# First layer's modulation rows loaded from GpSimd's queue, and the second half's first convolution weights split one step earlier

## The chip, the cores and the metric

One NeuronCore of a Trainium2 chip runs the whole program. The metric is the device time of one execution in microseconds (us), the median over several executions. TensorE is PE in the profile, VectorE is DVE, ScalarE is ACT, GpSimd is POOL, and SyncE, which here only issues DMAs, is SP. The letter q behind an engine's name (ACTq, SPq) marks what its queue does beside its computing: issuing a DMA or waiting on a semaphore.

## The reference

A two-layer decoder trunk over 1024 tokens of width 1024, in float32. Each layer is a token mixer and a squared-ReLU feed-forward network. Before each of them the residual stream is normalized (RMSNorm), scaled and shifted, and its result is gated. Scale, shift and gate come from a conditioning vector: `mod = silu(c) @ ada_w[i] + ada_b[i]`, six rows of 1024 for each layer. The first layer's mixer, the part that matters here, is

```python
u = h @ w_in                              # 1024 -> 2 x 1280
xb, gb = jnp.split(u, 2, axis=-1)
xc = causal_conv(xb, width 4) + conv_b
r, i = sigmoid(blockwise xc @ wr + br), sigmoid(blockwise xc @ wi + bi)
a = exp(-8 * r * softplus(-lam)); b = sqrt(1 - a*a) * (i * xc)
hs = scan(h_t = a_t * h_{t-1} + b_t)
y = (hs * gelu(gb)) @ w_out
```

## The kernel before, in words

**Tiling.** The 1024 tokens are two halves of 512, called h = 0 and h = 1. Activations lie transposed: a tile has 128 features on the partitions and 512 tokens along the row, 256 KB. Such tiles come from one pool of 54 buffers (tag `a`), which holds the residual stream, the mixer's inputs, the conv outputs, the mixer's outputs and the rows of `ada_w` on their way through.

**Products in three parts.** For float32 accuracy each operand is split in a high and a low part (`wh`, `wl` for weights). `mm3` (lines 343 to 347) issues three matmuls: high by high on line 345, high by low on 346, low by high on 347.

**Weights.** `weights` (line 299) loads a 512 KB block into one of three `raw` buffers over SP's queue (line 319), rounds it to `wh` on ACT (line 322), and subtracts to get `wl` (line 328). In the first layer's mixer the subtraction runs on DVE. `wh` and `wl` have five buffers each.

**The mixer** (`mixer0`, line 604). Its steps are written out in `plan` (line 1341): `c` is the conv branch of one of five blocks of 256 features, `g` the gelu branch, `l` the recurrence, `o` a part of the output product; the next digits are the blocks, the last one is the half. So `c01` is the conv branch of block 0 for half 1. A `c` or `g` step takes its weights from `wcols` (two blocks, `q` 0 and 1) and does 48 matmuls in `proj`. `nB` applies the norm to half 1: eight times a DVE instruction on line 96, one of ACT on line 97 and one of DVE on line 98, which give the eight inputs that every later step of half 1 needs. In the list around the change the order is `o20`, `nB`, `l40`, `c01`, `g01`, `o340`.

**Modulation as filler.** Rows of `ada_w` are not multiplied on PE in the mixer. `ada` (line 424) cuts a chunk of 1024 columns in eight steps; a step loads two 256 KB tiles (line 435) and DVE multiplies them by one entry of the condition each and adds (line 450 for the first step, line 452 for the others); `fin` turns the sum (PE, line 459) and reduces it (DVE, line 460). Each load is asked for one step ahead of its use. `pump` takes one such step from a list after each step of `plan`, two after steps 1 to 3. Four chunks of the first layer run during the mixer (64 loads); six of the second layer run later, during the feed-forward network (96 loads).

**What sets the order.** The kernel's text gives each instruction its engine and its place in the program. A scheduler then fixes, when the program is built, the order of every engine's queue, taking the earliest instruction in the program that is ready by its own model. On the chip each queue runs in that fixed order. Buffers of one tag are given out in the order of the program.

Of the kernel before, what the change touches and what calls it, by code (L numbers as in the profile page):

```python
# [21 lines left out]
P = 128  # L22
# [174 lines left out]
class Trunk:  # L197
# [226 lines left out]
    def ada(self, l, j, gain=None):  # L424

        nc = self.nc
        m = self.const.tile([P, KT], FT, name=f"mod{l}{j}")
        self.mod[l, j] = m
        st = {}

        def load(k):
            for c in range(2):
                st[k, c] = self.tile()
                o = j * D + c * 512
                nc.scalar.dma_start(st[k, c], self.i["ada_w"][l, k * P:(k + 1) * P, o:o + 512])

        self.loads += [lambda k=k: load(k) for k in range(KT)]

        def mac(k):
            if k == 0:  # L440
                st["acc"] = [self.tile(), self.tile()]
            while (k, 0) not in st:
                self.loads.pop(0)()
            if self.loads:
                self.loads.pop(0)()
            s = self.cond[:, k:k + 1]
            for c in range(2):
                r, a = st.pop((k, c)), st["acc"][c]
                if k == 0:
                    nc.vector.tensor_scalar(a, r, s, None, op0=OP.mult)  # L450
                else:
                    nc.vector.scalar_tensor_tensor(a, r, s, a, op0=OP.mult, op1=OP.add)  # L452

        def fin():
            t = self.small([P, KT], "adat")
            for c in range(2):
                ps = self.ps()
                for b in range(4):
                    nc.tensor.transpose(ps[:, b * P:(b + 1) * P], st["acc"][c][:, b * P:(b + 1) * P], self.ident)
                nc.vector.tensor_reduce(t[:, c * 4:c * 4 + 4], ps.rearrange("p (b k) -> p b k", b=4),  # L460
                                        axis=AX.X, op=OP.add)
            if gain is None:
                nc.vector.tensor_tensor(m, t, self.ada_b(l, j), op=OP.add)
            else:
                t2 = self.small([P, KT], "adat")
                nc.vector.tensor_tensor(t2, t, self.ada_b(l, j), op=OP.add)
                nc.vector.scalar_tensor_tensor(m, t2, 1.0, gain, op0=OP.add, op1=OP.mult)

        return [lambda k=k: mac(k) for k in range(KT)], fin
# [134 lines left out]
    def mixer0(self, hx, g1, tail, first, plan):  # L604
        nc, V, A, G = self.nc, self.nc.vector, self.nc.scalar, self.nc.gpsimd
# [6 lines left out]
        def wcols(c0):  # L612
            return [self.weights(w_in[0, q * 512:(q + 1) * 512, c0:c0 + 256].rearrange("(k p) c -> p k c", p=P),
                                 [4, 256], ("in", c0, q) if c0 not in (0, DR, 256) else None) for q in range(2)]

        def proj(W, h):
            pd = self.pd()
            pss = [pd[:, 0], pd[:, 1]]
            for kt in range(KT):
                wh, wl = W[kt // 4]  # L620
                for j in range(2):
                    s = slice(j * P, (j + 1) * P)
                    self.mm3(pss[j], (wh[:, kt % 4, s], wl[:, kt % 4, s]), hx[h][kt], kt == 0, kt == KT - 1)
            return pss

        def conv(u, h, pss=None):
            pss = pss or proj(wcols(u * 256), h)
            for j in range(2):
                f = 2 * u + j
                y = self.tmp("xc")  # L630
                A.activation(y, pss[j], AF.Identity, bias=self.convb(f), scale=self.convw(3, f))
                if h == 0:
                    A.copy(halo[:, f], pss[j][:, HT - 3:HT])
                for k in range(3):
                    d = 3 - k
                    V.scalar_tensor_tensor(y[:, d:], pss[j][:, 0:HT - d], self.convw(k, f), y[:, d:],  # L636
                                           op0=OP.mult, op1=OP.add)
                if h:
                    V.tensor_tensor(y[:, 0:3], y[:, 0:3], edge[:, f], op=OP.add)
                yh, yl = self.tileR(), self.tileR()  # L640
                A.copy(yh, y)
                V.tensor_tensor(yl, y, yh.bitcast(FT), op=OP.subtract)
                xc[u, j], xcs[u, j] = y, (yh, yl)

        def edges():

            t = self.small([P, 10, 3], "edge", 1)
            for k in range(3):
                n = 3 - k
                w = self.col[:, 136 + 10 * k:146 + 10 * k].rearrange("p (f o) -> p f o", o=1).to_broadcast([P, 10, n])  # L650
                d = t[:, :, 0:n] if k else edge
                V.tensor_tensor(d, halo[:, :, k:3], w, op=OP.mult)
                if k:
                    V.tensor_tensor(edge[:, :, 0:n], edge[:, :, 0:n], d, op=OP.add)
# [72 lines left out]
        conv(0, 0, first[0])  # L727
        gate(0, 0, first[1])
        conv(1, 0, first[2])
        for k, step in enumerate(plan):  # L730
            if callable(step):
                step()
            else:
                us = [int(u) for u in step[1:-1]]
                {"c": conv, "g": gate, "l": lru, "o": oproj}[step[0]](us if step[0] == "o" else us[0], int(step[-1]))
                if step == "c40":
                    edges()
            self.pump(2 if k in (1, 2, 3) else 1)
# [513 lines left out]
    def run(self):  # L1252
        tc = self.tc
        mod = self.mod = {}
        N = {}
        hm, hf = {}, {}

        def pool(st, name, bufs):
            return st.enter_context(tc.tile_pool(name=name, bufs=bufs))

        def sqs(key):
            def tail(h, m):
                if m == 0:
                    N[key, h] = Norm(self, h)
                N[key, h].sq(m)
            return tail
# [7 lines left out]
        def run(gen):  # L1274
            for _ in gen:
                pass
# [32 lines left out]
        with ExitStack() as st:  # L1309
            self.tp = pool(st, "tmp0", 18)  # L1310
            macs, fin = self.ada(0, 2)
            self.fill += macs
            self.ada_fill([(0, 4, self.gffn(0)), (0, 3), (0, 5)])
            self.loads.pop(0)()

            def nB():
                hm[1] = N["m0", 1].apply(mod[0, 1], mod[0, 0])

            def nA():
                hf[0] = N["f0", 0].apply(mod[0, 4], mod[0, 3])  # L1320

            def bA():
                N["f0", 0].bc()

            def stat0():
                N["f0", 0].stat()

            def f1a():
                self.drain()
                F.load1(0)  # L1330
                F.f1(0, 0)

            def f1b():
                def bcB():
                    N["f0", 1].bc()
                    hf[1] = N["f0", 1].apply(mod[0, 4], mod[0, 3])

                F.load1(1)
                F.f1(1, 0, mid={4: lambda: N["f0", 1].stat(), 6: bcB})

            plan = [lambda: self.second(), "g10", "l00", "c20", "l10", "g20", "c30", fin, "o010", "l20", "g30", "c40",
                    "l30", "g40", lambda: N["m0", 1].bc(), "o20", nB, "l40", "c01", "g01", "o340", "l01", "c11", stat0, "g11", "c21", "l11",
                    "g21", "c31", "o011", "l21", "g31", "c41", "l31", "g41", bA, "o21", nA, "l41", f1a, "o341", f1b]
            self.mixer0(hm, lambda: mod[0, 2], sqs("f0"), first, plan)
            self.drain()
            self.lo = [1]


            F.g2, F.tail = mod[0, 5], tail
            self.ada_fill([(1, 1, self.gmix(1)), (1, 0), (1, 2), (1, 4, self.gffn(1)), (1, 3), (1, 5)])  # L1350
            F.load2(0, 0)
            f2 = F.f2_steps([0], 0)
            for _ in range(4):
                next(f2)
            F.f1(0, 1), F.f1(1, 1)
            F.load2(0, 1)
            run(f2)
            F.f2([0], 1)
            for p in range(NJ):
                if p:  # L1360
                    F.load2(p, 0), F.load2(p, 1)
                    for h in range(2):
                        F.f2([p], h)
                if p + 2 < NJ:
                    F.load1(p + 2)
                    F.f1(p + 2, 0), F.f1(p + 2, 1)
            self.drain()
            F.twice = range(NJ, F.NP)
            F.single(0, NJ)
# [68 lines left out]
        with ExitStack() as st:  # L1438
# [72 lines left out]
            early = self.store(1, 0)  # L1511
# [38 lines left out]
```

## Time and profile before

| | us |
|---|---|
| runs: median of three | 2551.33 (2551.26 to 2557.24) |
| the profiled execution, time | 2558.93 |
| the profiled execution, span | 2557.0 |
| PE busy | 2435.1 |
| DVE busy | 1502.1 |
| ACT busy | 1227.8 |
| POOL busy | 797.6 |

The span runs from the first to the last instruction of the profiled execution. PE is busy for 95% of it, so little is to be had but where PE stands idle. Times in the trace are counted from the span's start; the first layer's mixer lies between about 70 and 500 us. A wait is put down to the instruction that released it: `PE pd L347 <- DVE wl L328` says that a matmul of line 347 waited for a `wl` that DVE wrote on line 328.

### The profile page before, as it was taken

What the parts mean: (1) busy time and instruction counts of PE and PEld (TensorE: products, weight loads), DVE (VectorE), ACT (ScalarE), POOL (GpSimd) and SP (SyncE); (2) the same over time, 40 slices, a digit from 0 to 9 for tenths busy, and PEclk for the clock granted to TensorE, in tenths of its full rate; (3) what the DMA queues carried; (4) which work ended last, traced back from release to release, by engine and by line L of the source; (5) the groups of instructions that cost most, each with busy time, mean ns of one, the idle gap of its engine ahead of it and who ended that gap; (6) DMA issues with size and microseconds to landing.
All of it is one profiled execution on the core that took longest, in us unless ns stands there. A gap on an engine that the chain in (4) does not pass through costs nothing. (4 is left out here: it accounts for less than half of the span.)

```text
span 2557.0 us, 30862 instructions
## 1 busy us (share of the span) xinstructions
PE 2435.1 (95%) x10954; PEld 1965.4 (77%) x10954; DVE 1502.1 (59%) x2905; ACT 1227.8 (48%) x2180; POOL 797.6 (31%) x507
## 2 busy tenths in 40 slices
PE   7998999999999999999987999999998999999999
PEld 6776787777788888788776777888887777788887
DVE  5888775788643412566677876555558875321212
ACT  3656465521211233235456667768634974423322
POOL 1000000022221243230238822322326994334442
PEclk8999999999999999999998999999999999999999
DMA  8564675356311577654321522322330114323231
GB/s 262 194 226 167 208 238 188 99 178 222 126 42 42 178 276 269 217 192 177 136 87 42 189 67 67 107 74 91 106 125 1 34 42 140 107 91 99 86 104 58
DMA packets 212284, 342.52 MB, mean 134 GB/s; under 512 B 19658, under 2 KB 123298, under 8 KB 212130
## 3 DMA queue, kind: packets, MB, share of 16 engines
q1 hardware_dynamic: 183184, 295.29, 34.2%
q10 hardware_dynamic: 28946, 45.27, 5.4%
q8 instruction: 86, 1.41, 0.2%
q14 instruction: 68, 0.56, 0.1%
HBM read 274.97 MB, written 65.54 MB: 133 GB/s over the span
## 5 line engine op out<-in xcount | busy, mean ns | idle before, releaser
L328 POOL TENSOR_TENSOR wl<-raw,wh 128x1024 fp32r<-128x1024 f32 (+2 forms) x194 | 470.7, 2433 | 1186.2 <-ACT wh L322 1169.3
L322 ACT CAST wh<-raw 128x1024 fp32r<-128x1024 f32 (+2 forms) x296 | 305.1, 1033 | 615.3 <-PE ps L346 238.8
L345 PE MATMUL ps<-a,wh 128*128 128x512 f32 x1152 | 461.0, 403 | 15.2 <-DVE a L723 7.5
L346 PE MATMUL ps<-a,wh 128*128 128x512 f32 x1152 | 459.2, 399 | 1.5 <-POOL a L1173 1.2
L347 PE MATMUL ps<-a,wl 128*128 128x512 f32 x1152 | 458.2, 399 | 0.7 <-DMA wl<-part 0.7
L345 PE MATMUL pd<-a,wh 128*128 128x512 f32 x1072 | 431.2, 404 | 12.2 <-DVE xc L636 9.4
L347 PE MATMUL pd<-a,wl 128*128 128x512 f32 x1072 | 429.5, 401 | 10.2 <-DVE wl L328 10.2
L346 PE MATMUL pd<-a,wh 128*128 128x512 f32 x1072 | 430.2, 402 | 2.0 <-DVE a L98 2.0
L168 DVE SCALAR_TENSOR_TENSOR a<-ps,mod,a 128x512 f32<-128x512 f32 x352 | 259.7, 746 | 262.8 <-PE ps L347 262.1
L345 PEld LDWEIGHTS ps<-a,wh 128*128 128x128 f32 x1152 | 218.5, 190 | 71.1 <-DVE a L723 7.9
L347 PEld LDWEIGHTS ps<-a,wl 128*128 128x128 f32 x1152 | 218.3, 190 | 54.4 <-DMA wl<-part 1.8
L346 PEld LDWEIGHTS ps<-a,wh 128*128 128x128 f32 x1152 | 218.4, 190 | 54.0 <-POOL a L1173 2.3
L345 PEld LDWEIGHTS pd<-a,wh 128*128 128x128 f32 x1072 | 204.6, 191 | 63.2 <-issue 6.5
L347 PEld LDWEIGHTS pd<-a,wl 128*128 128x128 f32 x1072 | 204.8, 191 | 60.7 <-DVE wl L328 11.1
L346 PEld LDWEIGHTS pd<-a,wh 128*128 128x128 f32 x1072 | 205.3, 191 | 53.2 <-DVE a L98 3.4
L1141 POOL TENSOR_SCALAR s<-s,rr 128x128 f32<-128x128 f32 (+7 forms) x128 | 225.9, 1782 | 35.8 <-DVE rr L1139 25.2
L345 PE MATMUL ps<-hid,wh 128*128 128x512 f32 x512 | 204.9, 400 | 9.6 <-DVE a L168 6.8
L346 PE MATMUL ps<-hid,wh 128*128 128x512 f32 x512 | 203.6, 398 | 0.0
L347 PE MATMUL ps<-hid,wl 128*128 128x512 f32 x512 | 203.6, 398 | 0.0
L1019 ACT ACTIVATE signs<-sc,tc 128x384 int8<-128x384 f32 (+5 forms) x186 | 164.0, 882 | 77.3 <-DVE tc L1034 66.0
L452 DVE SCALAR_TENSOR_TENSOR a<-a,cond,a 128x512 f32<-128x512 f32 x140 | 113.5, 840 | 40.7 <-DMA a<-in_ada_w_dram 40.3
L146 DVE TENSOR_TENSOR a<-r,a 128x512 fp32r<-128x512 f32 x64 | 46.8, 754 | 141.7 <-ACT a L145 140.4
(271 smaller groups left out, 3684.1 us busy)
## 6 DMA issues: line engine op xcount, KB each, us to landing
raw<-in_ffn_w_dram SPq DMA_DIRECT2D x192, 512.0 KB, 3.7
a<-in_ada_w_dram ACTq DMA_DIRECT2D x160, 256.0 KB, 3.4
part<-wl SPq DMA_DIRECT2D x69, 512.0 KB, 3.2
wl<-part SPq DMA_DIRECT2D x69, 512.0 KB, 4.3
part<-wh SPq DMA_DIRECT2D x40, 512.0 KB, 2.8
wh<-part SPq DMA_DIRECT2D x40, 512.0 KB, 3.8
raw<-in_a_w_in_dram SPq DMA_DIRECT2D x34, 512.0 KB, 4.9
raw<-in_a_w_out_dram SPq DMA_DIRECT2D x20, 512.0 KB, 4.1
```

The lines of the kernel that those rows point to most:

```text
L146: nc.any.tensor_tensor(ql, r, qh.bitcast(FT), op=OP.subtract)
L168: nc.vector.scalar_tensor_tensor(xt, ps, self.g2[:, m:m + 1], xt, op0=OP.mult, op1=OP.add)
L322: nc.scalar.copy(wh, raw)
L328: eng.tensor_tensor(wl, raw, wh.bitcast(FT), op=OP.subtract)
L345: pe.matmul(out, wh, xh, start=start, stop=False)
L346: pe.matmul(out, wh, xl, start=False, stop=False)
L347: pe.matmul(out, wl, xh, start=False, stop=stop)
L452: nc.vector.scalar_tensor_tensor(a, r, s, a, op0=OP.mult, op1=OP.add)
L1019: A.activation(self.signs[:, 0:L], sc, AF.Sign, bias=0.0 if neg is None else neg.bitcast(FT), accum_out=n)
L1141: G.tensor_scalar(sl[e][:, 0:L], sl[e][:, 0:L], r[:, e:e + 1], None, op0=OP.mult)
```

## The change

Two edits. The loads of `ada_w` for the first layer are issued by GpSimd's queue in place of ScalarE's; those of the second layer stay where they are. A new step `w01` between `o20` and `nB` calls `wcols` for block 0 (load, `wh` and `wl` of both weight blocks), and `c01` takes these tiles in place of calling `wcols` itself. As the list has one step more, one more filler step is taken before the steps behind it.

```diff
-                nc.scalar.dma_start(st[k, c], self.i["ada_w"][l, k * P:(k + 1) * P, o:o + 512])
+                (nc.scalar if l else nc.gpsimd).dma_start(st[k, c], self.i["ada_w"][l, k * P:(k + 1) * P, o:o + 512])
...
+        ready = {}
+
+        def early(u, h):
+
+            ready[u] = wcols(u * 256)
+
         def conv(u, h, pss=None):
-            pss = pss or proj(wcols(u * 256), h)
+            pss = pss or proj(ready.pop(u, None) or wcols(u * 256), h)
...
-                {"c": conv, "g": gate, "l": lru, "o": oproj}[step[0]](us if step[0] == "o" else us[0], int(step[-1]))
+                {"w": early, "c": conv, "g": gate, "l": lru, "o": oproj}[step[0]](us if step[0] == "o" else us[0], int(step[-1]))
...
-                    "l30", "g40", lambda: N["m0", 1].bc(), "o20", nB, "l40", "c01", "g01", "o340", "l01", "c11", stat0, "g11", "c21", "l11",
+                    "l30", "g40", lambda: N["m0", 1].bc(), "o20", "w01", nB, "l40", "c01", "g01", "o340", "l01", "c11", stat0, "g11", "c21", "l11",
```

## Rows read from the trace of the kernel before

**Rows 1.** The page: span, and busy time of each engine.

```profile
span 2557.0 us, 30862 instructions
PE 2435.1 (95%) x10954; PEld 1965.4 (77%) x10954; DVE 1502.1 (59%) x2905; ACT 1227.8 (48%) x2180; POOL 797.6 (31%) x507
```

**Rows 2.** PE's waits, 100 to 300 us: us in total, times, longest.

```profile
PE pd L347 <- DVE wl L328: 9.6, 1, 9.6
PE ps L345 <- DVE a L723: 6.7, 3, 3.8
PE pd L345 <- DVE xc L636: 5.4, 1, 5.4
```

**Rows 3.** Busy time by stretch: length, PE, PEld, DVE, ACT, POOL, granted clock, DMA, GB/s.

```profile
125.00:300.00 175.00, 153.20 (x627) 121.24 (x626) 144.35 (x216) 95.72 (x132) 0.00 (x0) 0.93 0.58 196
235.00:270.00 35.00, 23.61 (x91) 18.49 (x89) 33.07 (x50) 18.76 (x26) 0.00 (x0) 0.80 0.32 104
300.00:420.00 120.00, 119.22 (x517) 95.58 (x516) 77.94 (x123) 71.72 (x96) 1.49 (x1) 1.00 0.69 229
```

**Rows 4.** DVE's longest wait in total, 100 to 300 us.

```profile
DVE a L452 <- DMA a<-in_ada_w_dram: 23.6, 15, 4.9
```

**Rows 5.** PE in order of time: start, length, line; idle before it.

```profile
138.74 0.63 PE L346 MATMUL pd<-a,wh 128*128 128x512 f32 x1
...
237.80 1.03 PE L459 MATMUL ps<-ident,a 128*128 128x128 f32 x8
...
258.58 0.79 PE L347 MATMUL pd<-a,wl 128*128 128x512 f32 x1 [9.61 <-DVE wl L328]
...
281.95 0.39 PE L345 MATMUL ps<-a,wh 128*128 128x512 f32 x1
```

**Rows 6.** DVE in order of time.

```profile
132.70 1.43 DVE L452 SCALAR_TENSOR_TENSOR a<-a,cond,a 128x512 f32<-128x512 f32 x2 [3.19 <-DMA a<-in_ada_w_dram]
...
253.36 0.74 DVE L98 SCALAR_TENSOR_TENSOR a<-ns,mod,a 128x512 fp32r<-128x512 f32 x1
...
257.31 2.35 DVE L328 TENSOR_TENSOR wl<-raw,wh 128x1024 fp32r<-128x1024 f32 x2
...
263.08 1.21 DVE L328 TENSOR_TENSOR wl<-raw,wh 128x1024 fp32r<-128x1024 f32 x1
...
275.14 0.75 DVE L452 SCALAR_TENSOR_TENSOR a<-a,cond,a 128x512 f32<-128x512 f32 x1 [4.90 <-DMA a<-in_ada_w_dram]
```

**Rows 7.** DVE by group, 195 to 270 us: busy, mean ns; idle before.

```profile
L452 DVE SCALAR_TENSOR_TENSOR a<-a,cond,a 128x512 f32<-128x512 f32 x12 | 8.7, 747 | 5.2 <-DMA a<-in_ada_w_dram 5.2
```

**Rows 8.** Line 435, 70 to 420 us: ns min/median/max, first and last start.

```profile
L435 ACTq DMA_DIRECT2D a<-in_ada_w_dram x64: 334/389/1166, 74.9 to 387.8; - x64
L435 ACTq EVENT_SEMAPHORE  x14: 17/17/17, 102.1 to 387.3; - x14
DMA to landing us min/median/max: 2.8/3.8/7.8
```

**Rows 9.** ACT and its queue in order of time.

```profile
126.98 2.97 ACTq L435 DMA_DIRECT2D a<-in_ada_w_dram  x4
...
219.16 2.01 ACT L322 CAST wh<-raw 128x1024 fp32r<-128x1024 f32 x2
...
267.93 1.05 ACT L322 CAST wh<-raw 128x1024 fp32r<-128x1024 f32 x1 [0.58 <-DMA raw<-in_a_w_out_dram]
267.95 0.82 ACTq L435 DMA_DIRECT2D a<-in_ada_w_dram  x2
```

**Rows 10.** POOL by group, 26 to 500 us: busy, mean ns; idle before.

```profile
L76 POOL TENSOR_TENSOR rs<-rs,mhalf 128x4 f32<-128x4 f32 x2 | 2.5, 1268 | 299.3 <-DVE rs L74 299.3
```

**Rows 11.** Lines 328 on POOL and 452 on DVE, 500 to 700 us.

```profile
L328 POOL TENSOR_TENSOR wl<-raw,wh x17: 2385/2590/3727, 503.6 to 697.9; 128x1024 fp32r<-128x1024 f32 x17
L452 DVE SCALAR_TENSOR_TENSOR a<-a,cond,a x84: 735/744/2893, 529.4 to 669.7; 128x512 f32<-128x512 f32 x84
```

**Rows 12.** Line 435, 100 to 300 us.

```profile
L435 ACTq DMA_DIRECT2D a<-in_ada_w_dram x46: 334/389/1166, 101.7 to 294.9; - x46
```

## The prediction, as it was put on record

> **What bounds the kernel now.** I first read the page for the engines' shares: PE is busy for 2435.1 of 2557.0 us [rows 1], so a change pays only where PE stands idle. PE's waits come next. Between 100 and 300 us, in the first layer's mixer, PE waits five times, 21.7 us in all, and each time for DVE: 9.6 us for a `wl`, 6.7 us for updates of the residual stream, 5.4 us for a conv output [rows 2]. The busy times by stretch show who is late. From 235 to 270 us DVE works 33.07 of 35 us and PE 23.61; from 300 to 420 us PE works 119.22 of 120 us, so what is won before 300 us isn't handed back there [rows 3]. DVE's own waits say why it is late: of its idle time between 100 and 300 us, 23.6 us in 15 waits go to one thing, the landing of `ada_w` tiles for the filler on line 452 [rows 4].
>
> A wait also slows PE behind it. At 138.74 us, just after the wait of 5.4 us, a matmul takes 0.63 us, where one with PE busy before takes 0.39 (281.95 us) [rows 5]; eight more of 0.63 follow. In 235 to 270 us the granted clock is 0.80 on average, part of the time at the lower of the two levels, 1.2 for 2.4 GHz [rows 3]. As 9 matmuls by about 0.2 us this costs some 1.8 us a long wait.
>
> **Part one, the loads on POOL's queue.** It moves 64 DMA issues of 256 KB from ACT to POOL, 389 ns each in the middle and 1166 at most, and of the semaphore waits ahead of them none took over 17 ns [rows 8]. So when ACT reached a load, its buffer was free, or within 0.8 us of it: the moment of issue came from the load's place in ACT's queue. At 267.95 us the pair starts right behind a cast on line 322 that had waited for its own weights [rows 9]. It lands 7 us later, and DVE, which has the filler next in its order, stands idle 4.90 us until 275.14 us [rows 6]. By the addresses in the program of before, that buffer was last read by the transposes at 237.80 us [rows 5], some 29 us ahead of the issue. The same holds for the four issues at 126.98 us [rows 9] and DVE's wait of 3.19 us until 132.70 us [rows 6].
>
> POOL has little else here: two small powers for norms between 26 and 500 us, with 299.3 us of idle time ahead of them [rows 10]. They are what is queued behind the loads; `stat0` emits the second, well behind loads whose buffers come free long before, so I cost its delay at nothing. If that cover went, DVE, which uses its result next, would wait as long.
>
> What a load costs on POOL no row shows. From below it is ACT's shortest issue, 0.33 us [rows 8]; from above POOL's usual large instruction, 2.59 us [rows 11]; I take 1.27, the mean of those powers [rows 10], the nearest in kind, as both carry little data. Even at 2.59 us a load lands 2.2 us later after its issue, against an issue that can move up by more than the longest wait, 4.9 us. So I take the 23.6 us of DVE's waits as gone, and two of them count for PE. The 3.19 us ahead of PE's wait of 5.4 us come off it: **-3.2 us**. The 5.2 us that DVE waits between 195 and 270 us [rows 7] stand ahead of PE's next waits, and DVE is all but full from there to 264 us: every DVE result there comes **5.2 us** earlier. ACT also loses 64 x 0.389 = 25 us of issuing; it isn't the bound, so I count nothing.
>
> **Part two, the weights ahead of the norm.** No instruction is added; two loads on SP, two casts on ACT and two subtractions on DVE move up past `nB` and `l40`. `c01`'s casts run at 219.16 us already [rows 9], but DVE makes both `wl` only at 257.31 us, behind the 16 instructions of the norm, and PE waits 9.61 us for the first until 258.58 us [rows 5, 6]. Moved up, they take 2.35 us of DVE [rows 6] ahead of the norm, so the norm's last result (253.36 + 0.74 = 254.1) comes at 256.5 by itself. On SP the two loads now go ahead of `l40`'s gate weights, which PE needs for the 24 matmuls that end as its wait of 9.61 us begins; the loads ahead of them are issued as soon as a `raw` buffer is free, some 40 us before, so nothing for that. On ACT the casts keep about their place.
>
> Next late is `g01`. Its first `wl` ends at 263.08 + 1.21 = 264.3 us [rows 6]. PE started `g01` at about 270.8: its 48 matmuls end at 281.95 us [rows 5], at 120/517 = 0.232 us each [rows 3]. So part two by itself is worth at most 270.8 - 264.3 = **6.5 us**, then PE waits for `g01`'s `wl` in place of `c01`'s.
>
> **The sum.** Together: 3.2 + 5.2 + 6.5 = 14.9 us. One wait stays ahead of `g01`. PE's wait began at 258.58 - 9.61 = 249.0 [rows 5]; 8.4 us earlier is 240.6, and the 44 matmuls left of `c01` at 0.232 us end by 250.8, behind the norm's last result at 256.5 - 8.4 = 248.1. `g01`'s `wl` is there at 264.3 - 8.4 = 255.9. So PE falls to the lower clock once more and pays 1.8 us that `g01` did not pay before: **-13 us**. Against the profiled span that is 2544; the runs' median is 2551.33, 7.6 us under the profiled execution's time, and I take the difference off the median: **2538 us**.
>
> A rule of the Trainium skill speaks against this sum: DMA: Bandwidth & Descriptors, section "Issuing engines are not separate DMA queues", has it that another issuing engine saves only the time of issuing. By that rule part one would be worth nothing on PE's path; the first rival below prices it. The trace agrees with the rule on bandwidth only: what DVE waits for here is a load stuck in a queue [rows 9].
>
> **The rivals.**
>
> *Only part two works, 2545 to 2549.* POOL's loads land no earlier, because each costs POOL more than I think or stands behind another one's buffer, or the 7 us to landing at 268 us are a busy moment of the DMA engines. For it: landing takes up to 7.8 us [rows 8]. Against it: the middle is 3.8, and the buffers are free early. Then 2 to 6.5 us are left. With it goes the case that the scheduler's new order sets an equal wait elsewhere, since DVE is full and any wait moved up moves others down by 2.35 us: no change. Together 28%.
>
> *More, 2525 to 2531.* The new order also brings `g01`'s `wl` ahead of the recurrence of `l40`, since its raw buffers come free some 35 us earlier. Then PE goes from `c01` into `g01` without a wait, and nearly all of 21.7 us and three slow stretches of 1.8 go: 20 to 26 us. 14%.
>
> *Slower, about 2579.* POOL's descriptor work holds DVE up. The row that shows the two engines in each other's way is DVE's line 452 beside POOL's subtractions: 2893 ns for 744 [rows 11]. If each issue held DVE for the 1.27 us that I give it, the 46 issues between 100 and 300 us [rows 12] would cost DVE 58 us. From 125 to 300 us it has 175 - 144.35 = 30.7 us of idle time to take it from [rows 3], so PE would lose some 28 us. It decides the sign from 30.7/46 = 0.67 us per issue on. Against it: an issue carries no data through POOL, as the subtraction does. 12%.
>
> SBUF — State Buffer, section "Who interferes with whom", of the Trainium skill bears on this: a DVE instruction with two SBUF inputs meets only a GpSimd instruction that reads SBUF, while descriptor writing is locked out by DVE's two-port modes. By it DVE would not be held up here; with the slower case struck out the forecast would gain its chance. No run of before shows a load from GpSimd.
>
> **How the numbers follow.** The forecast, 8 to 20 us faster, has 46%. Faster by over 0.3%, about what a measurement of this kernel can tell from no change (7.7 us, under 2543.7), takes the forecast and the larger gain, and a little of the first rival's upper end: 0.61. Within 0.3%: 0.27. Slower by over 0.3%: 0.12. The range runs from the larger gain (2526) to just past no change (2555); it leaves out the slower case and the far end of the larger gain. The forecast's own range is 2531 to 2543.
>
> **What would show it.** Right: line 435 on POOL, its loads landing well before line 452 runs; DVE's 23.6 us in 15 waits shrunk to under 3; PE's wait of 5.4 us near 138 us under 3; no wait of 9.6 us ahead of `c01`, but one of up to 6 us ahead of `g01`; the end of `g01` some 13 us before 281.95. Wrong: DVE's line 452 still waiting for `ada_w`, DVE instructions between 100 and 300 us longer than 0.75 us, or a new wait of PE for the norm's results on line 98, or one after 300 us where PE now has nearly none.

## The result, and the profile after

The changed kernel takes 2528.57 us (median of four runs, 2527.51 to 2532.5) against 2552.49 us before: a ratio of 0.9908, 95% interval 0.9892 to 0.9923. A second set of six runs, beside the last experiments below, gave 2532.94 against 2551.46, ratio 0.9926 (0.9911 to 0.9942). So the change saves 19 to 24 us. The prediction said 13, in a range of 2526 to 2555; the sign and the range hold. The first set lies in its rival "more" (20 to 26 us faster), the second, 18.5 us faster, near the upper end of the forecast's own 8 to 20.

The two profiled executions are 30.2 us apart (2557.0 and 2526.8 us of span). Some 8 us of that belong to those two executions and not to the change: the one of before lies 7.6 us over its median. To read the stages without it, I count matmuls in a stretch of fixed length: at 0.232 us each [rows 3], what PE does more of in a stretch is what it wins there.

The page after, span and busy times:

```profile
span 2526.8 us, 30938 instructions
...
PE 2422.8 (96%) x10954; PEld 1953.7 (77%) x10954; DVE 1504.5 (60%) x2905; ACT 1227.4 (49%) x2180; POOL 828.8 (33%) x571
```

POOL has 31 us more than in [rows 1], ACT's busy time is the same, since issuing isn't counted as busy there. PE's waits after, 100 to 300 us (us in total, times, longest):

```profile
PE ps L345 <- DVE a L729: 3.7, 3, 2.8
PE ps L345 <- DVE adat L460: 1.1, 1, 1.1
PE pd L345 <- ACT a L97: 0.7, 1, 0.7
...
```

With two shorter ones, 0.4 and 0.3, they sum to 6.2 us where [rows 2] has 21.7 for DVE alone. (From line 626 on, a line of after is six higher: L729 is L723 of before.) No wait for a `wl` is left, and none for a conv output near 138 us. Busy times by stretch, with the columns of [rows 3]:

```profile
60.00:125.00 65.00, 59.40 (x264) 47.73 (x264) 55.72 (x94) 43.49 (x78) 8.65 (x15) 0.95 0.73 246
125.00:300.00 175.00, 168.67 (x719) 132.45 (x718) 156.84 (x239) 107.29 (x147) 22.60 (x41) 0.99 0.60 203
235.00:270.00 35.00, 34.65 (x148) 27.29 (x147) 30.52 (x43) 21.20 (x29) 3.24 (x6) 1.00 0.66 223
300.00:420.00 120.00, 120.00 (x518) 96.63 (x517) 71.47 (x113) 71.42 (x94) 4.32 (x8) 1.00 0.64 216
```

From 125 to 300 us PE does 719 matmuls for 627: 92 x 0.232 = 21.3 us won. Ahead of it some is lost; the stretch from 60 to 125 us of the kernel before was

```profile
60.00:125.00 65.00, 60.48 (x273) 48.85 (x272) 52.73 (x93) 41.27 (x72) 1.04 (x1) 0.95 0.61 211
```

which makes 264 for 273, 2.1 us. So some 19 us are won by 300, in line with the runs. From 235 to 270 us it is busy throughout, at a granted clock of 1.00 for 0.80; behind 300 us nothing is handed back. DVE's wait for the filler's tiles, then line 435 with its landing times, then the filler itself:

```profile
DVE a L452 <- DMA a<-in_ada_w_dram: 4.0, 1, 4.0
```

```profile
L435 POOL DMA_DIRECT2D a<-in_ada_w_dram x62: 538/538/599, 97.2 to 351.8; - x62
...
DMA to landing us min/median/max: 2.8/5.5/8.0
```

```profile
L452 DVE SCALAR_TENSOR_TENSOR a<-a,cond,a x56: 739/746/752, 101.9 to 367.8; 128x512 f32<-128x512 f32 x56
```

DVE's 23.6 us in 15 waits [rows 4] are 4.0 us in one, near 168 us; the prediction had said under 3. A load costs POOL 0.54 us and lands in 5.5 us in the middle, later than the 3.8 from ACT's queue [rows 8], but it is asked for earlier. DVE's filler takes 746 ns: DVE is not held up.

How the second part works is seen on DVE around the norm of half 1:

```profile
208.36 1.23 DVE L328 TENSOR_TENSOR wl<-raw,wh 128x1024 fp32r<-128x1024 f32 x1 [0.84 <-ACT wh L322]
...
211.43 1.22 DVE L328 TENSOR_TENSOR wl<-raw,wh 128x1024 fp32r<-128x1024 f32 x1
...
242.51 0.75 DVE L98 SCALAR_TENSOR_TENSOR a<-ns,mod,a 128x512 fp32r<-128x512 f32 x1
...
243.83 2.36 DVE L328 TENSOR_TENSOR wl<-raw,wh 128x1024 fp32r<-128x1024 f32 x2
...
247.43 1.22 DVE L328 TENSOR_TENSOR wl<-raw,wh 128x1024 fp32r<-128x1024 f32 x1
...
259.13 2.33 DVE L705 TENSOR_TENSOR_SCAN hs<-la,tg 128x512 f32<-128x512 f32 x2
```

The first two are `c01`'s, 47 to 49 us ahead of where they were [rows 6]. The pair behind the norm is `l40`'s `wl` and the first of `g01`, the next one the second of `g01`. All of these stand ahead of `l40`'s recurrence (line 705). Before, `l40`'s `wl` was made ahead of the norm, and the recurrence (there line 699) stood ahead of `g01`'s first `wl` at 263.08 us [rows 6]:

```profile
210.90 1.21 DVE L328 TENSOR_TENSOR wl<-raw,wh 128x1024 fp32r<-128x1024 f32 x1
...
260.79 2.33 DVE L699 TENSOR_TENSOR_SCAN hs<-la,tg 128x512 f32<-128x512 f32 x2
```

So two splits changed places around the norm: `c01`'s went ahead of it, `l40`'s behind it. PE's order changed with them. Before, it did `l40`'s 24 matmuls and then waited for `c01`'s `wl`; after, `c01`'s 48 (to `pd`) run from 233.27 us on and `l40`'s (to `ps`) behind them:

```profile
245.63 0.40 PE L347 MATMUL pd<-a,wl 128*128 128x512 f32 x1
245.86 0.40 PE L347 MATMUL ps<-a,wl 128*128 128x512 f32 x1
```

While PE does `c01`, DVE ends the norm and makes the next `wl`; the recurrence, which needs what ACT makes of `l40`'s matmuls, comes after that. That this order of PE is why `g01`'s first `wl` stands ahead of the recurrence is argued from the traces, not tried by itself.

For `g01`'s second block the traces also show a chain of buffers. Before, `c01`'s blocks kept their raw buffers until DVE subtracted them at 257 us. SP asked for `g01`'s first block at 212.14 us, when `l40`'s `wl` had been made; the second could be asked for only behind `c01`'s, and its cast on ACT waited for it:

```profile
212.14 0.37 SPq L319 DMA_DIRECT2D raw<-in_a_w_in_dram  x1
...
258.59 0.37 SPq L319 DMA_DIRECT2D raw<-in_a_w_in_dram  x1
```

```profile
262.88 1.05 ACT L322 CAST wh<-raw 128x1024 fp32r<-128x1024 f32 x1 [5.42 <-DMA raw<-in_a_w_in_dram]
```

After, SP asks for `g01`'s first block at 209.62 us, right behind `c01`'s first subtraction, for the second some 3 us later, and ACT has cast it by 228.6:

```profile
209.62 3.43 SPq L319 DMA_DIRECT2D raw<-in_a_w_in_dram  x2
```

```profile
227.51 1.05 ACT L322 CAST wh<-raw 128x1024 fp32r<-128x1024 f32 x1 [3.57 <-PE ps L346]
```

The second block comes 46 us earlier, the first only 2.5: what moved the first `wl` was the order, and not a buffer.

So, behind a wait of 0.7 us at its start, PE runs through `c01`, `l40` and `g01` without a wait. The first matmul behind `g01`, the counterpart of the one at 281.95 us [rows 5]:

```profile
260.39 0.40 PE L345 MATMUL ps<-a,wh 128*128 128x512 f32 x1
```

It comes 21.6 us earlier, of which some 4.6 us lie in the first 60 us (258 matmuls for 238; see the last section).

### The profile page after: what moved, and what is told of

Same layout as the page of the kernel before. It is cut to its first block, busy times and chain, and to the rows that moved or that the text cites. A ratio compares the mean times of both kernels' runs of the same rounds, so it can differ in the third digit from the quotient of the medians.

```text
span 2526.8 us, 30938 instructions
## 1 busy us (share of the span) xinstructions
PE 2422.8 (96%) x10954; PEld 1953.7 (77%) x10954; DVE 1504.5 (60%) x2905; ACT 1227.4 (49%) x2180; POOL 828.8 (33%) x571
## 5 line engine op out<-in xcount | busy, mean ns | idle before, releaser
L345 PEld LDWEIGHTS ps<-hid,wh 128*128 128x128 f32 x512 | 96.7, 189 | 37.8 <-DVE a L168 10.3
```

The lines of the kernel that those rows point to most:

```text
L345: pe.matmul(out, wh, xh, start=start, stop=False)
```

## The experiments

The expectations name their theories by letters. **Q**: the loads were late because of their place in ACT's queue. **I**: another queue saves no more than time of issuing. **O**: what counts is the scheduler's new order, or the filler step that the longer list adds. **R**: the early split works through the raw buffers, which brings `g01`'s weights ahead of the recurrence. **M**: what the prediction missed of the gain comes from `g01`'s `wl` standing ahead of the recurrence. The other letters are told where they stand.

### Each part alone

The loads alone, on the kernel before:

```diff
-                nc.scalar.dma_start(st[k, c], self.i["ada_w"][l, k * P:(k + 1) * P, o:o + 512])
+                (nc.scalar if l else nc.gpsimd).dma_start(st[k, c], self.i["ada_w"][l, k * P:(k + 1) * P, o:o + 512])
```

> Part one alone: the first layer's ada_w loads on POOL, no step w01. Theory Q (the loads were late because of their place in ACT's queue): 9 to 14 us faster than before; DVE's wait for ada_w between 100 and 300 us falls from 23.6 us to under 6, PE's wait of 5.4 us near 138 us goes, and PE still waits 4 to 10 us for c01's wl. Theory I (another queue saves only the time of issuing, 25 us of an engine that is not the bound): within 4 us of before. Theory O (the scheduler's new order, above all the one more filler step, makes the gain): within 4 us.

Measured: 2541.37 us, ratio 0.9961 (0.9946 to 0.9976), 10.2 us faster (6.1 to 13.8). PE's waits from 100 to 300 us, its work by stretch, and DVE's wait:

```profile
PE pd L347 <- DVE wl L328: 5.4, 1, 5.4
PE ps L345 <- DVE a L723: 4.1, 2, 2.6
...
```

```profile
125.00:300.00 175.00, 164.66 (x686) 130.58 (x685) 151.73 (x227) 104.74 (x147) 17.21 (x32) 0.96 0.60 200
235.00:270.00 35.00, 29.63 (x120) 23.46 (x119) 32.41 (x49) 20.05 (x28) 3.23 (x6) 0.90 0.54 177
```

```profile
DVE a L452 <- DMA a<-in_ada_w_dram: 5.0, 1, 5.0
```

The wait of 5.4 us near 138 us is gone whole, `c01`'s went from 9.6 to 5.4, the residual updates from 6.7 to 4.1. Part one pays because DVE no longer stands idle for its tiles, as Q says.

The split alone, on the kernel before (the diff of the change without line 435):

> Part two alone: step w01 ahead of the norm, the ada_w loads stay on ACT. Theory Q: 5 to 9 us faster than before; DVE's wait for ada_w stays near 20 us, the wait of 9.6 us ahead of c01 goes and one of 2 to 6 us stands ahead of g01. Theory I: 18 us faster or more, nearly the whole of the change's 24 us, as part one would give nothing. Theory O: as much as the empty step in its place gives, and a few us more.

Measured: 2537.01 us, ratio 0.9944 (0.9931 to 0.9957), 14.5 us faster (11 to 17.6), more than Q and the prediction gave it; I's 18 us or more is not reached either. PE's longest wait of 100 to 300 us, its work, then DVE's waits and order:

```profile
PE pd L345 <- DVE xc L642: 5.5, 1, 5.5
```

```profile
125.00:300.00 175.00, 163.03 (x688) 128.46 (x687) 153.80 (x232) 107.17 (x149) 0.59 (x1) 0.97 0.63 210
```

```profile
DVE a L452 <- DMA a<-in_ada_w_dram: 11.3, 11, 3.1
```

```profile
249.93 2.35 DVE L328 TENSOR_TENSOR wl<-raw,wh 128x1024 fp32r<-128x1024 f32 x2
253.52 1.22 DVE L328 TENSOR_TENSOR wl<-raw,wh 128x1024 fp32r<-128x1024 f32 x1
...
265.18 2.33 DVE L705 TENSOR_TENSOR_SCAN hs<-la,tg 128x512 f32<-128x512 f32 x2
```

Part one's wait of 5.5 us stays, as it should. No wait for a `wl` is left, as `g01`'s subtractions stand ahead of the recurrence here too. DVE's waits for tiles halve, to 11.3 us, without any load moved to another queue, where Q had them stay near 20. Together the parts are 24.7 us by themselves, against 19 to 24 for the whole, and the intervals don't tell these apart. The traces do: from 125 to 300 us part one alone gives 59 matmuls more, part two 61, and both together 92. The parts overlap, as each takes from `c01`'s wait of 9.6 us, which can go only once.

### The longer list alone

```diff
-                    "l30", "g40", lambda: N["m0", 1].bc(), "o20", nB, "l40", "c01", "g01", "o340", "l01", "c11", stat0, "g11", "c21", "l11",
+                    "l30", "g40", lambda: N["m0", 1].bc(), "o20", lambda: None, nB, "l40", "c01", "g01", "o340", "l01", "c11", stat0, "g11", "c21", "l11",
```

> The kernel before with an empty step where w01 stands, so that one more filler step is taken there and each later one comes a step earlier. Theory Q and theory I: within 5 us of before, either way. Theory O: over 8 us faster.

Measured: 2551.43 us, ratio 1.0 (0.9989 to 1.0011). The filler step taken earlier is worth nothing, to within 3 us, and with it falls the half of O that rests on it. The other half, a new order, comes back in what part two does.

### Early loads that stay on ACT

```diff
-            self.loads.pop(0)()
+            for _ in range(3):
+                self.loads.pop(0)()
```

> The kernel before with the first layer's ada_w loads still issued by ACT, but asked for three filler steps ahead of their use and not one (four tiles more in flight). Theory Q: ACT's place in its queue no longer matters, 8 to 14 us faster, about as e1; DVE's wait for ada_w between 100 and 300 us under 6 us. Theory I: ACT issues as much as before, so within 3 us. Theory O: not told apart.

Measured: 2547.24 us, ratio 0.9981 (0.9971 to 0.999), 4.3 us faster (2.6 to 7.4): below Q's forecast, and above I's by less than the interval. The profile shows both a gain and a loss. PE's longest wait, 60 to 300 us, and its work:

```profile
PE pd L345 <- DVE xc L636: 7.9, 1, 7.9
```

```profile
125.00:300.00 175.00, 162.43 (x671) 128.22 (x669) 151.35 (x226) 102.36 (x140) 0.00 (x0) 0.96 0.62 208
```

Between 125 and 300 us PE does 44 matmuls more than before, 10.2 us, while ACT still issues every load. That is most of the 59 that POOL's queue gave, so most of the cost was lateness, and not ACT's time of issuing. That the issuing costs nothing isn't shown: no run takes the issues off ACT and leaves the loads late. But PE's wait at 83 us, behind the start of the mixer, has grown from 4.0 to 7.9 us, and a new one of 3.8 us stands ahead of line 459. Loads that come early for the filler may stand ahead of work that the start needs; that was not tried by itself.

### Another queue than POOL's

The kernel before with the loads on SP's queue:

```diff
-                nc.scalar.dma_start(st[k, c], self.i["ada_w"][l, k * P:(k + 1) * P, o:o + 512])
+                (nc.scalar if l else nc.sync).dma_start(st[k, c], self.i["ada_w"][l, k * P:(k + 1) * P, o:o + 512])
```

> The kernel before with line 435's 64 loads of the first layer on SP's queue, where the weight loads are, in place of POOL's. Theory Q (a load was late because of the instructions ahead of it in ACT's queue, and POOL's gains because that queue is empty): SP's queue is no empty one, its weight loads wait for raw buffers and the modulation loads now stand behind them, so DVE's waits for ada_w tiles between 100 and 300 us stay above 12 us (23.6 before, 5.0 with the loads on POOL) and the time is within 5 us of before, 2546 to 2557, or slower. Theory I2 (what pays is that ACT no longer spends 25 us on issuing, whatever queue takes the loads over): about the 10 us of the loads on POOL, 2538 to 2545.

Measured: 2536.01 us, ratio 0.9942 (0.9929 to 0.9954), 15.8 us faster (11.7 to 18.1). Q's forecast is refuted; I2's is passed by 2 us. DVE's wait, and SP's queue in order of time:

```profile
DVE a L452 <- DMA a<-in_ada_w_dram: 1.4, 3, 0.7
```

```profile
215.62 4.77 SPq L435 DMA_DIRECT2D a<-in_ada_w_dram  x8
250.77 6.80 SPq L319 DMA_DIRECT2D raw<-in_a_w_out_dram  x3
```

SP's queue does wait for raw buffers, for 30 us up to 250.77. But the scheduler put eight loads ahead of that wait, where ACT's pair came at 267.95 us [rows 9]. So a queue need not be empty, as POOL's is: in ACT's it came behind casts that had to wait for their own weights [rows 9]. By itself the time fits I2 better than Q; against I2 stand the 44 matmuls won by loads that came early on ACT's own queue. Why SP alone gives 5 us more than POOL alone I did not settle; the intervals overlap, and DVE's waits are 1.4 us for 5.0.

Both parts with SP in place of POOL:

> The changed kernel with the first layer's modulation loads on SP's queue in place of POOL's; the early split stays. Theory A (what part one removes is ACT's queue: any queue that asks for the tiles well ahead of the filler does the same, as SP's alone gained 15.8 us and POOL's alone 10.2): as fast as the changed kernel, 2524 to 2531. Theory B (on SP the loads of weights and of modulation rows stand in each other's way once c01's weights are loaded early): slower than the changed kernel by 4 us or more, 2533 to 2541.

Measured: 2532.21 us, ratio 0.9925 (0.991 to 0.9939), beside 2532.94 for the changed kernel in the same set. 1.2 us over A's forecast, but the same time as the changed kernel: with the split early, POOL and SP are worth the same. By themselves the loads on SP and the split are worth 15.8 + 14.5 = 30.3 us, together 19.2: here the overlap of the parts is plain.

### Where the split has to stand

The changed kernel with `w01` behind the norm:

```diff
-                    "l30", "g40", lambda: N["m0", 1].bc(), "o20", "w01", nB, "l40", "c01", "g01", "o340", "l01", "c11", stat0, "g11", "c21", "l11",
+                    "l30", "g40", lambda: N["m0", 1].bc(), "o20", nB, "w01", "l40", "c01", "g01", "o340", "l01", "c11", stat0, "g11", "c21", "l11",
```

> The changed kernel with the step w01 set behind the norm nB and still ahead of l40. Theory R (what counts is that the split stands ahead of l40: its raw buffers are asked for and come free earlier, so that g01's weights come ahead of l40's recurrence): the time of the changed kernel within 3 us, 2526 to 2532. Theory N (it has to stand ahead of the norm's 16 instructions on DVE): PE waits for c01's wl again, for part of the 9.6 us that it did, and at least 4 us of part two's 14.5 are lost, 2532.5 or more.

Measured: 2533.43 us, ratio 0.9937 (0.9924 to 0.9951): 4.9 us over the changed kernel's first four runs. By the time alone this is N's forecast (2532.5 or more) and 1.4 us over R's; but PE waits for no `wl`. So the changed kernel was run again:

> The changed kernel as it is, beside the others on the same chip, since its time was known from four runs. Theory R (the split may stand on either side of the norm, as long as it is ahead of l40): the median comes to lie between 2529 and 2533, so that the 5 us to the kernel with the split behind the norm shrink to under 4. Theory N (the place ahead of the norm counts): 2526 to 2529, and those 5 us stay.

Measured: 2532.94 us (2528.35 to 2536.13). The difference is 0.5 us, as R has it. But in the kernel with `w01` behind the norm the scheduler set `c01`'s subtractions at 213 and 216 us all the same, some 20 us ahead of the norm's first instruction:

```profile
213.26 1.22 DVE L328 TENSOR_TENSOR wl<-raw,wh 128x1024 fp32r<-128x1024 f32 x1 [0.85 <-ACT wh L322]
...
235.47 2.06 DVE L96 SCALAR_TENSOR_TENSOR ns<-a,mod,ps 128x512 f32<-128x512 f32 x3
```

So the place of `w01` in the list, ahead of the norm or behind it, is not what counts; ahead of `l40` it stands in both. Whether the subtractions have to run ahead of the norm on DVE this run can't tell, as they did in both.

### `g01`'s weights held back

The first subtraction for `g01` gets its factor -1 from what `l40`'s recurrence leaves, so it can't be made earlier:

```diff
-        eng.tensor_tensor(wl, raw, wh.bitcast(FT), op=OP.subtract)
+        self.minus = eng.scalar_tensor_tensor(wl, wh.bitcast(FT), self.minus, raw, op0=OP.mult, op1=OP.add) and None if self.minus is not None else eng.tensor_tensor(wl, raw, wh.bitcast(FT), op=OP.subtract) and None
...
+        def held(c):
+            self.minus = self.small([P, 1], "minus", 1); V.tensor_scalar(self.minus, last[:, 8:9], 0.0, -1.0, op0=OP.mult, op1=OP.add)
+            return wcols(c)
...
-            pss = pss or proj(wcols(DR + u * 256), h)
+            pss = pss or proj(held(DR) if (u, h) == (0, 1) else wcols(DR + u * 256), h)
```

> The changed kernel in which the first subtraction of g01's weights takes its factor -1 from a value that l40's recurrence leaves, so that DVE can make this wl only behind the recurrence, as the prediction had it; three DVE instructions of 128x1 are added, about 0.3 us. Theory M (the part of the gain that the prediction missed comes from g01's wl standing ahead of the recurrence): PE waits ahead of g01 for a wl again, 4 to 10 us, its clock falls there, and the time rises by 5 to 12 us over the changed kernel, to 2533 to 2541. Theory K (the missed part comes from elsewhere, from c01's split alone or from ACT's queue): PE has something else to do or catches up, and the time stays within 3 us of the changed kernel.

Measured: 2546.75 us, ratio 0.9979 (0.9969 to 0.9988): 13.8 to 18.2 us over the changed kernel, more than M's 5 to 12. (The trace has one added DVE instruction of 0.14 us, not three.) PE's two new waits, its work, and DVE's order:

```profile
PE pd L347 <- DVE wl L328: 11.1, 1, 11.1
...
PE ps L345 <- ACT wh L322: 3.6, 1, 3.6
```

```profile
235.00:270.00 35.00, 20.28 (x75) 15.47 (x74) 27.12 (x44) 17.00 (x24) 3.23 (x6) 0.74 0.27 90
```

```profile
257.52 2.33 DVE L705 TENSOR_TENSOR_SCAN hs<-la,tg 128x512 f32<-128x512 f32 x2
...
264.56 1.28 DVE L328 SCALAR_TENSOR_TENSOR wl<-wh,minus,raw 128x1024 fp32r<-128x1024 f32 x1
```

K falls. With `c01`'s split early and `g01`'s first `wl` late, three quarters of the gain is gone: the two waits, and the clock, 0.74 in this stretch for 1.00. That is more than the lateness of `g01` by itself: the scheduler set the held subtraction behind `c01`'s first conv updates too, and took a part of `o340` ahead of `g01`. The wait of 3.6 us is for `o340`'s first weights, whose cast runs at 251.64 us, no later than in the changed kernel (252.30); PE has only come to them early. How the 13.8 to 18.2 us divide was not tried.

### `g01`'s weights asked for still earlier

The changed kernel with a second step, `v01`, which calls `wcols` for `g01` ahead of `l40`:

```diff
+        def earlyg(u, h):
+
+            ready["g", u] = wcols(DR + u * 256)
...
-            pss = pss or proj(wcols(DR + u * 256), h)
+            pss = pss or proj(ready.pop(("g", u), None) or wcols(DR + u * 256), h)
...
-                    "l30", "g40", lambda: N["m0", 1].bc(), "o20", "w01", nB, "l40", "c01", "g01", "o340", "l01", "c11", stat0, "g11", "c21", "l11",
+                    "l30", "g40", lambda: N["m0", 1].bc(), "o20", "w01", nB, "v01", "l40", "c01", "g01", "o340", "l01", "c11", stat0, "g11", "c21", "l11",
```

> The changed kernel with g01's weights asked for and split ahead of l40 as well, in a step of their own behind the norm. Theory M (g01's wl is ahead of l40's recurrence by itself already, and PE waits for nothing ahead of g01): nothing left to win there, the time of the changed kernel within 3 us, and slower where l40's own weights come later for it. Theory V (the split stands on DVE's way wherever its place is set by buffers, and an earlier place still pays): 3 us or more faster than the changed kernel.

Measured: 2543.11 us, ratio 0.9967 (0.9954 to 0.998), 10 to 15 us over the changed kernel. V falls, and of M's two forecasts it is the slower one. A new wait of PE, at 274 us, and two behind 300 us, where the changed kernel has none:

```profile
PE ps L345 <- ACT a L714: 3.6, 1, 3.6
...
PE pd L345 <- DVE xc L646: 2.2, 1, 2.2
PE pd L347 <- DVE wl L328: 2.0, 1, 2.0
```

A place in the three raw buffers that one step is given is taken from the steps behind it: `l40`'s gate weights, asked for at 198.29 us in the changed kernel, are asked for at 217.33 here. That the three waits come from this is likely and was not tried, say with a fourth raw buffer.

### Twice the issues on POOL

```diff
-                (nc.scalar if l else nc.gpsimd).dma_start(st[k, c], self.i["ada_w"][l, k * P:(k + 1) * P, o:o + 512])
+                for n in ([0] if l else [0, 256]): (nc.scalar if l else nc.gpsimd).dma_start(st[k, c][:, n:n + (512 if l else 256)], self.i["ada_w"][l, k * P:(k + 1) * P, o + n:o + n + (512 if l else 256)])
```

> The changed kernel in which each load of line 435 for the first layer is made of two loads of half the width, so POOL issues 128 loads in place of 64. Theory H (POOL's issuing is hidden, and holds no other engine up): POOL's busy time on line 435 doubles by about 34 us, DVE's line 452 stays at 0.75 us, and the time is that of the changed kernel within 3 us. Theory D (writing descriptors on POOL holds DVE up): DVE instructions beside it get longer, and the second 46 issues between 100 and 300 us cost PE at least 5 us.

Measured: 2534.6 us, ratio 0.9934 (0.9919 to 0.995), 1.7 us over the changed kernel of the same set. Line 435, and the filler on DVE:

```profile
L435 POOL DMA_DIRECT2D a<-in_ada_w_dram x124: 536/538/771, 101.1 to 356.8; - x124
```

```profile
L452 DVE SCALAR_TENSOR_TENSOR a<-a,cond,a x56: 739/744/752, 107.2 to 372.2; 128x512 f32<-128x512 f32 x56
```

H holds: twice the issues, DVE's instructions as long as before, the time within 3 us. The price of an issue on POOL does not follow the bytes: it is 538 ns for half the width too, with the same 128 rows in each load.

## Why the prediction was right, and where its size failed

**What bounds the kernel** was right. PE's waits between 100 and 300 us were what could be won, and what was won there was not handed back behind 300.

**Part one** was right in its mechanism and nearly in its size: -3.2 and -5.2, together -8.4, against -10.2 measured. That the sum comes so near is in part luck. Its wait near 138 us (5.4) went whole and not by 3.2; `c01`'s fell by 4.2, not 5.2; the residual updates fell by 2.6; and PE's wait at the mixer's start grew from 4.0 to 5.1 us, which the prediction did not see. POOL's price of 1.27 us was too high, 0.54 measured. That was without effect, as doubling the issues showed.

**Part two** is the term that was mis-sized: at most -6.5, against -14.5 measured. The step that failed is "Next late is `g01`. Its first `wl` ends at 263.08 + 1.21 = 264.3 us". It moved `c01`'s instructions and left the order of DVE and of PE as it was. But that order is set anew for each program: PE does `c01` ahead of `l40`, and both of `g01`'s subtractions stand ahead of the recurrence, at 245.0 and 247.4 us. The prediction named this as its rival "more" and gave it 14%. The cause that it named, raw buffers that come free early, holds for `g01`'s second block, 46 us earlier; the first, on which its term rests, was asked for only 2.5 us earlier, and there the new order did it. Held back by force, `g01`'s weights took away three quarters of the gain, side effects included.

**The wait ahead of `g01`** with 1.8 us of lower clock did not come, for the same reason. The waits taken out by part two, 21.7 to 11.9 us, are 9.8, and with 1.8 for the one slow stretch that goes along, 11.6; the interval of the measurement reaches from 11 to 17.6.

**The rivals.** "Only part two works" fell: part one alone is worth 10.2 us. By the rule in DMA: Bandwidth & Descriptors, section "Issuing engines are not separate DMA queues", of the Trainium skill, another issuing engine saves only the sequencer's time. The trace does not agree with this for a queue that runs in order: POOL gave 10.2 us and SP 15.8, and loads that were early on ACT's own queue won 10.2 us of work between 125 and 300. What the queue changes is above all what stands ahead of the load. "Slower" fell: DVE's filler stayed at 0.75 us, with 64 issues and with 128. SBUF — State Buffer, section "Who interferes with whom", of the Trainium skill has it that a DVE instruction with two SBUF inputs, like this one, meets only GpSimd instructions that read SBUF. Nothing here speaks against it, 744 to 746 ns with the loads on POOL and 750 without; whether an issue on POOL reads SBUF no run shows.

**The chances.** The forecast's own range, 2531 to 2543, holds the second set (2532.94) and not the first (2528.57). 14% for "more" was too little: the prediction itself said that the raw buffers come free some 35 us earlier, and with the order of DVE set anew that was enough to weigh it more. Of its signs, no wait ahead of `c01`, no lengthened DVE instruction and no new wait behind 300 us came as said; the wait ahead of `g01` did not come.

No kernel here beats the changed one by more than can be measured; the one with both parts on SP is its equal.

## What to carry to other kernels

A load's queue matters by what stands ahead of it: take loads for later work off an engine whose instructions wait for their neighbours, and put them on any queue that reaches them early. When a step is moved, follow its buffers as well as its instructions: who gets the freed buffer next, and what is that step waiting for? Where a scheduler fixes the order, don't hold the old order fixed in the sum; and where buffers are few, a claim moved ahead can be paid by the next one. Parts that shorten the same wait don't add up: measure them alone and together.

## What the runs showed of the hardware

A load of 256 KB lands later after its issue from POOL (5.5 us in the middle) than from ACT (3.8 us), but SP's loads take 6.0 us as well. Why the two earlier queues have the later landings was not tried. DVE's waits fell all the same, from 23.6 to 4.0 us with POOL and 1.4 with SP, as the loads are asked for so much ahead.

The first 60 us, up to where the mixer starts, are not the same in each execution of one and the same kernel. Here are the changed kernel's two profiled executions, with the columns of the stretches above:

```profile
0.00:60.00 60.00, 45.90 (x258) 39.52 (x258) 36.69 (x113) 19.82 (x31) 11.23 (x36) 0.94 0.93 281
```

```profile
0.00:60.00 60.00, 46.99 (x235) 40.64 (x236) 33.80 (x104) 17.73 (x28) 10.57 (x36) 0.86 0.87 257
```

The granted clock is 0.94 in one and 0.86 in the other, with 258 and 235 matmuls done, some 5 us apart. Differences of a few us between two profiles of this kernel mean nothing until this stretch is taken off; why it differs was not tried.
